# Per-channel scale-and-bias steps of a hybrid mixer kernel, on ScalarE instead of VectorE

## The chip, the cores and the metric

The kernel runs on one core of a Trainium2 chip. The metric is the device time of one execution in microseconds (us); the median of three runs of the kernel before is 2065.13 us (2061.42 to 2069.36). A core has a matrix engine (TensorE, PE in the profile, with its weight loads shown as PEld), a vector engine (VectorE, DVE), an engine for activation functions (ScalarE, ACT), GpSimd (POOL) and a queue that issues most DMAs (SyncE, SP). Each engine executes its own list of instructions strictly in the order of the list, and waits on semaphores for the others.

## The reference, cut to what matters

Two groups of tokens (128 context tokens and 512 latent ones, 640 columns in all) go through two layers. In each layer a normalised input of 1024 features is projected to some 11,800 columns, which feed four mixers (retention, RG-LRU, gated DeltaNet and HGRN2, 4 heads or blocks of 128 channels each, forward and backward); a projection of each, gated, is summed, projected again and added to the input. Two places matter here: the convolutions over four neighbouring tokens, and the gate of HGRN2.

```python
def conv_centred(x, w):
    xp = jnp.pad(x, ((0, 0), (CONV_LEFT, CONV_K - 1 - CONV_LEFT), (0, 0)))
    return sum(xp[:, j:j + n] * w[j] for j in range(CONV_K))
...
xb = conv_centred(bx, lru_conv_w[l]) + lru_conv_b[l]
qkv = jax.nn.silu(conv_centred(jnp.concatenate([cq, ck, cv], -1), gdn_conv_w[l]))
...
k_in = (1.0 - lb) * jax.nn.sigmoid(-zf)
f_gate = lb + (1.0 - lb) * jax.nn.sigmoid(zf)
log_f = jnp.log(jnp.maximum(f_gate, 1e-30))
```

With t = tanh(zf / 2), both gate values are affine in t, with one factor and one addend per channel: k = hb - hb * t and f = ha + hb * t.

## The kernel before, in words

Features lie on the 128 partitions and tokens along the row, so a tile of one head is 128 x 640 (128 x 644 with the padding of a convolution). The large products (projection, branch and output) run as jobs of 128 output features: a 512 KB weight tile is loaded, split into a rounded part (`whi`, an ACT copy, L359) and a rest (`wlo`, a DVE subtraction, L361), and multiplied in 48 matmuls, 24 for columns 0 to 383 and 24 for columns 384 to 639 (L376, output `pj`, two PSUM buffers in turn). After each half ACT copies the result out of PSUM, often through a tanh (`mg`, `p_df` at L521, `p_dq` and `p_bz` at L515, where DVE then multiplies at L516), or plainly (`p_ck`, `p_cq`, `p_cv`, `p_bx` at L507 to L510).

Between these matmuls stand the small ones of the mixers (`m`, L297, and transposes, L301). Two lanes run beside the jobs: the DeltaNet heads in one, the HGRN2, retention and RG-LRU heads in the other. The kernel is written as generators that yield where a result has to come back; a clock that counts PE work decides which lane goes on next. The order of each engine's list is then set by the tile framework's scheduler, which moves instructions against each other within the bounds of their dependencies. All engines' lists are fixed before the run.

The change touches `conv` (L848), which starts with a product by one factor per channel (L851; L853 with an addend too) and adds three more taps on DVE (L855), and the function `after` inside `hgrn_in` (L1114), which makes the two gate tiles from the tanh `th` at L1117 and L1118 and then bounds one of them from below (L1119). `conv` is called 12 times in a layer for DeltaNet and 4 times for RG-LRU (16 in a layer, 32 in all), `after` 8 times in a layer (16 in all). Other names in the rows: `gS`, `vk`, `r`, `gvn` are tiles of the DeltaNet chain over five blocks of tokens (L1066 to L1096), whose products with `cs` and `kt` alternate with DVE and ACT steps; `lt` is a gate tile of RG-LRU (L1376), `lxh` and `lgh` the operands of its matmuls; `dfull` is a tile of the DeltaNet inverse, `mjunk` a dot product of the next layer's modulation; `wide` and `wpart` belong to the first jobs of a layer.

Of the kernel before, what the change touches and what calls it, by code (L numbers as in the profile page):

```python
# [26 lines left out]
AF = mybir.ActivationFunctionType  # L27
OP = mybir.AluOpType
# [10 lines left out]
CONVW = SC + 3 + SS + 1  # L39
# [40 lines left out]
def hybrid_kernel(ctx: ExitStack, tc: tile.TileContext, I, O):  # L80
    nc = tc.nc
    V, G, A, PE = nc.vector, nc.gpsimd, nc.scalar, nc.tensor
# [69 lines left out]
    def UP(shape=None, dt=F32, name="p"):  # L152
        return up.tile([128, T] if shape is None else shape, dt, tag="pu", name=name, bufs=NPU)
# [44 lines left out]
    def small(w, name):  # L198
        return cp.tile([128, w], F32, name=name)
# [13 lines left out]
    def softplus(out, x, w):  # L213
# [11 lines left out]
    lg, cpos, cneg, gbh, ea, ha, hb, hbn, ghg, ghh = (small(w, n) for n, w in (  # L225
        ('lg', 16), ('cpos', 16), ('cneg', 16), ('gbh', 32), ('ea', 16), ('ha', 16), ('hb', 16), ('hbn', 16), ('ghg', 2), ('ghh', 2)))
# [547 lines left out]
    def layer(l, hh, hl):  # L774
# [6 lines left out]
        def proj_to(S, key, name, i, evac, shape=None, after=None):  # L781
            def run(hi, lo):
                x = UP(shape, name="p_" + name)
                yield from product(hi, lo, hh, hl, evac(x), halves=halves)
                if after:
                    after(x)
                S[key] = x
            return Job(I['w_in'][l, CIDX[name, i]], run, cost=2 if name == 'df' else 1)
# [59 lines left out]
        def conv(xp, wcol, dst, bias=None):  # L848

            if bias is None:  # L850
                V.tensor_scalar(dst[:, :CONVW], xp[:, :CONVW], wcol(0), None, op0=OP.mult)  # L851
            else:
                V.tensor_scalar(dst[:, :CONVW], xp[:, :CONVW], wcol(0), bias, op0=OP.mult, op1=OP.add)  # L853
            for j in (1, 2, 3):
                V.scalar_tensor_tensor(dst[:, :CONVW], xp[:, j:j + CONVW], wcol(j), dst[:, :CONVW],  # L855
                                       op0=OP.mult, op1=OP.add)
# [4 lines left out]
        def gdn_conv(h, S, nm):  # L861
            cs = U([128, PADW], name="cs")
            widx = {'cq': 0, 'ck': 4, 'cv': 8}[nm] + h
            conv(S.pop(nm), lambda j: P('gconv_w', l, 12 * j + widx, 1), cs)
            free(1)
            th = U([128, PADW], name="cth")
            A.activation(th[:, :CONVW], cs[:, :CONVW], AF.Tanh, scale=0.5)
            V.scalar_tensor_tensor(cs[:, :CONVW], th[:, :CONVW], 1.0, cs[:, :CONVW], op0=OP.add, op1=OP.mult)
            return cs
# [242 lines left out]
        def hgrn_in(h, S):  # L1112
            def gates(d):
                def after(th):  # L1114
                    c = 8 * l + 4 * d + h
                    k = S['k', d] = UP(name="hk%d" % d)
                    V.tensor_scalar(k, th, hbn[:, c:c + 1], hb[:, c:c + 1], op0=OP.mult, op1=OP.add)  # L1117
                    V.tensor_scalar(th, th, hb[:, c:c + 1], ha[:, c:c + 1], op0=OP.mult, op1=OP.add)  # L1118
                    V.tensor_scalar(th, th, 1e-30, None, op0=OP.max)  # L1119
                return after  # L1120
            return [proj_to(S, 'q', 'dq', h, ev_silu2)] + \
                [proj_to(S, ('f', d), 'df', 4 * d + h, ev_tanh, after=gates(d)) for d in range(2)] + \
                [proj_to(S, 'v', 'di', h, ev_copy)]
# [220 lines left out]
        def lru_mix(c, S):  # L1344
            yield lambda: 'x' in S
            xb = U([128, PADW], name="lxb")
            conv(S['x'], lambda j: P('conv_w', l, 4 * j + c, 1), xb, bias=P('conv_b', l, c, 1))
            free(1)
            gr = U([128, 256], name="lgr")
# [481 lines left out]
```

## Time and profile before

| | |
|---|---|
| median of three runs | 2065.13 us |
| the profiled execution | 2065.96 us, of which the span of the profile is 2063.8 us |
| PE busy | 2026.3 us, 98% of the span |
| PEld busy | 1967.7 us, 95% |
| DVE busy | 1401.8 us, 68% |
| ACT busy | 950.3 us, 46% |
| POOL busy | 77.5 us, 4% |

Shares are averages over the span. Matmuls overlap in the records, and the ends of matmuls are modelled, so how fast PE really goes is read from how many matmuls stand in a stretch of time, not from the busy share alone. What an engine waited for is named by the semaphore that came last.

### The profile page before, as it was taken

The numbers are of one execution on the slowest core, as the hardware profiler recorded it, in microseconds if no ns is written. First come the engines' busy times: TensorE is split into PE (matmuls) and PEld (weight loads), VectorE is DVE, ScalarE is ACT, GpSimd is POOL, SyncE is SP. The second block draws the span as 40 slices with busy tenths as digits, with TensorE's granted clock in tenths as the row PEclk, the third lists the DMA queues.
The fourth block names the chain that finished last, engine by engine and source line by source line (L and its number), as shares of the span: only waits on it lengthen the run. The fifth ranks groups of instructions, "written<-read, shape, count | busy, mean of one in ns | idle before, by whom it ended". The sixth has DMA issues, their size and how long they took to land.

```text
span 2063.8 us, 42790 instructions
## 1 busy us (share of the span) xinstructions
PE 2026.3 (98%) x17362; PEld 1967.7 (95%) x17362; DVE 1401.8 (68%) x3164; ACT 950.3 (46%) x2036; POOL 77.5 (4%) x195
## 2 busy tenths in 40 slices
PE   7999999999999999999999999999999999999997
PEld 5999999999999999999989999999999999999997
DVE  5799998757756954458568656945784686552764
ACT  4443365456537445422344437444643654372221
POOL 0000000001000000000000000000100000000000
PEclk9999999999999999999999999999999999999999
DMA  8236643223323232455422322232332233243632
GB/s 322 80 128 193 187 150 93 93 94 100 100 76 104 84 107 94 143 190 179 144 73 92 94 81 92 92 97 69 123 93 77 78 118 93 96 153 117 212 130 94
DMA packets 133305, 244.20 MB, mean 118 GB/s; under 512 B 44068, under 2 KB 60148, under 8 KB 132980
## 3 DMA queue, kind: packets, MB, share of 16 engines
q1 hardware_dynamic: 131956, 238.85, 35.6%
q8 instruction: 136, 2.23, 0.5%
q10 hardware_dynamic: 1152, 2.62, 0.3%
q14 instruction: 61, 0.50, 0.1%
HBM read 204.15 MB, written 37.27 MB: 117 GB/s over the span
## 4 chain that ended last, share of the span: by engine, by line
PE 89%; DMA 3%; DVE 3%; ACT 3%; issue 1%; SPq 1%; POOL 0%; DVEq 0%; ACTq 0%
PE pj L376 74%; PE m L297 13%; PE m L301 2%; PE wide L384 1%; DMA dct<-d_dr 1%; DMA wss<-in_w_ss 1%; DVE mjunk L630 1%; DMA d_dr<-sW 0%; ACT dfull L1002 0%; DVE wlo L361 0%; ACT whi L359 0%; DMA R<-gc 0%; DMA par<-in_params 0%; ACT lt L1376 0%; DMA tab<-in_tables 0%
## 5 line engine op out<-in xcount | busy, mean ns | idle before, releaser
L376 PE MATMUL pj<-hh,whi 128*128 128x256 f32 (+2 forms) x2896 | 912.9, 315 | 2.9 <-DVE p_dz L516 1.1
L376 PE MATMUL pj<-hl,whi 128*128 128x256 f32 (+2 forms) x2896 | 905.9, 313 | 0.1
L376 PE MATMUL pj<-hh,wlo 128*128 128x256 f32 (+1 forms) x2880 | 899.4, 312 | 0.0
L376 PEld LDWEIGHTS pj<-hh,whi 128*128 128x128 f32 (+1 forms) x2896 | 547.5, 189 | 9.0 <-issue 1.5
L376 PEld LDWEIGHTS pj<-hl,whi 128*128 128x128 f32 (+1 forms) x2896 | 547.8, 189 | 3.7 <-issue 2.0
L376 PEld LDWEIGHTS pj<-hh,wlo 128*128 128x128 f32 x2880 | 545.5, 189 | 3.2 <-issue 1.9
L359 ACT ACTIVATE whi<-wraw 128x1024 fp32r<-128x1024 f32 x230 | 243.4, 1058 | 302.6 <-PE pj L376 259.6
L361 DVE TENSOR_TENSOR wlo<-wraw,whi 128x1024 fp32r<-128x1024 f32 x228 | 278.7, 1223 | 141.1 <-ACT whi L359 137.6
L376 PE MATMUL pj<-bl,whi 128*128 128x384 f32 (+1 forms) x512 | 158.1, 309 | 0.0
L376 PE MATMUL pj<-bh,whi 128*128 128x384 f32 (+1 forms) x512 | 158.0, 309 | 0.0
L376 PE MATMUL pj<-bh,wlo 128*128 128x384 f32 (+1 forms) x512 | 157.5, 309 | 0.0
L376 PEld LDWEIGHTS pj<-bl,whi 128*128 128x128 f32 x512 | 96.3, 188 | 0.0
L376 PEld LDWEIGHTS pj<-bh,whi 128*128 128x128 f32 x512 | 96.3, 188 | 0.0
L376 PEld LDWEIGHTS pj<-bh,wlo 128*128 128x128 f32 x512 | 96.2, 188 | 0.0
L521 ACT ACTIVATE mg<-pj 128x384 f32<-128x384 f32 (+1 forms) x128 | 54.9, 429 | 80.3 <-PE pj L376 76.8
L630 DVE SCALAR_TENSOR_TENSOR mjunk<-wm,cs 128x512 bf16<-128x512 f32 x128 | 87.9, 686 | 2.2 <-DMA wm<-in_w_mod 1.6
L1376 ACT ACTIVATE lt<-m,gbh 64x322 f32<-64x322 f32 x128 | 67.3, 526 | 31.2 <-PE m L297 29.7
L376 PE MATMUL pj<-yl,whi 128*128 128x256 f32 (+1 forms) x256 | 78.9, 309 | 0.0
L376 PE MATMUL pj<-yh,whi 128*128 128x384 f32 (+1 forms) x256 | 78.8, 310 | 0.0
L376 PE MATMUL pj<-yh,wlo 128*128 128x256 f32 (+1 forms) x256 | 78.0, 309 | 0.0
L543 ACT ACTIVATE junk<-m 128x128 bf16<-128x128 f32 x160 | 44.5, 278 | 61.0 <-PE m L297 53.9
L967 DVE TENSOR_TENSOR sW<-sW,sLt 128x126 f32<-128x126 f32 (+22 forms) x248 | 62.8, 253 | 8.5 <-POOL sW L960 3.7
(394 smaller groups left out, 2892.0 us busy)
## 6 DMA issues: line engine op xcount, KB each, us to landing
wraw<-in_w_in SPq DMA_DIRECT2D x184, 512.0 KB
mg<-mg SPq DMA_DIRECT2D x96, 320.0 KB
wm<-in_w_mod SPq DMA_DIRECT2D x64, 256.0 KB
wraw<-in_w_branch SPq DMA_DIRECT2D x32, 512.0 KB
R<-gc SPq DMA_DIRECT2D x32, 320.0 KB
braw<-br SPq DMA_DIRECT2D x32, 320.0 KB
wss<-in_w_ss SPq DMA_DIRECT2D x32, 256.0 KB
wraw<-in_w_out SPq DMA_DIRECT2D x16, 512.0 KB
```

The lines of the kernel that those rows point to most:

```text
L297: return PE.matmul(out, lhsT, rhs, **k)
L301: return PE.transpose(out, in_, idn)
L359: A.activation(hi, raw, AF.Copy)
L361: behind(lambda: (lo_on or j.lo_on or V).tensor_sub(lo, raw, hi.bitcast(F32)), after)
L376: PE.matmul(ps[:m, :b - a], w[:, k0 + k], r[k][:, a:b], start=(k + n == 0), stop=(k == nk - 1 and n == len(ops) - 1))
L384: PE.matmul(ps[:m, :b - a], w[:, k], r[k][:, a:b], start=(k + n == 0), stop=(k == nk - 1 and n == (2 if lo else 1)))
L521: A.activation(dst[:, a:b], ps, AF.Tanh, scale=0.5)
L543: A.activation(junk, src3[:, t, :], AF.Square, accum_out=ss[:, t:t + 1])
L630: V.scalar_tensor_tensor(junk, w, 1.0, cs[2 * g + a], op0=OP.mult, op1=OP.mult, accum_out=macc[l][:, c, 2 * g + a:2 * g + a + 1])
L967: V.tensor_tensor(tv, X3[:, :m, i:i + 1].to_broadcast([128, m, n]), L3[:, i:i + 1, i + 1:].to_broadcast([128, m, n]), op=OP.mult)
L1376: A.activation(gts[g][i:i + 64, sx], ps[64 * g:64 * g + 64, b], AF.Tanh, scale=0.5, bias=gbh[i:i + 64, bi + 4 * g:bi + 4 * g + 1])
```

## The change

The first tap of `conv` and the two affine steps of `after` are taken from DVE's list and put on ACT's, as activations Copy or Identity with scale and bias from the same columns. The other three taps and the bound stay on DVE.

```diff
         def conv(xp, wcol, dst, bias=None):
             if bias is None:
-                V.tensor_scalar(dst[:, :CONVW], xp[:, :CONVW], wcol(0), None, op0=OP.mult)
+                A.activation(dst[:, :CONVW], xp[:, :CONVW], AF.Copy, scale=wcol(0))
             else:
-                V.tensor_scalar(dst[:, :CONVW], xp[:, :CONVW], wcol(0), bias, op0=OP.mult, op1=OP.add)
+                A.activation(dst[:, :CONVW], xp[:, :CONVW], AF.Identity, scale=wcol(0), bias=bias)
...
                 def after(th):
-                    V.tensor_scalar(k, th, hbn[:, c:c + 1], hb[:, c:c + 1], op0=OP.mult, op1=OP.add)
-                    V.tensor_scalar(th, th, hb[:, c:c + 1], ha[:, c:c + 1], op0=OP.mult, op1=OP.add)
+                    A.activation(k, th, AF.Identity, scale=hbn[:, c:c + 1], bias=hb[:, c:c + 1])
+                    A.activation(th, th, AF.Identity, scale=hb[:, c:c + 1], bias=ha[:, c:c + 1])
                     V.tensor_scalar(th, th, 1e-30, None, op0=OP.max)
```

The scheduler orders every engine's list anew, so small matmuls, evacuations and splits stand at other places too. Three places follow.

ACT's list at the start of layer 0, as a piece of the difference: `p_cq` is the second projection's evacuation, `beta` a small tile of DeltaNet gates.

```order
 L508 ACTIVATE p_cq<-wide 128x256
 L510 ACTIVATE p_cq<-wide 128x256
+L851 ACTIVATE cs<-p_ck,par 128x644
 L810 ACT_TABLE_LOAD
 L810 ACTIVATE beta<-m_767 128x40
```

The first tap of the first convolution now stands on ACT, behind the evacuations of `p_cq` and ahead of a table load.

PE's list in the chain of the first DeltaNet head, before: `m_2697` and `m_2700` are the products from which the two directions' new `gS` are made, `m_2730` the first product that reads one of them.

```order
L297 MATMUL m_2697<-vk,kt 128x128
L376 MATMUL pj<-hh,whi 128x256
L376 MATMUL pj<-hl,whi 128x256
L376 MATMUL pj<-hh,wlo 128x256
L376 MATMUL pj<-hh,whi 128x256
L376 MATMUL pj<-hl,whi 128x256
L376 MATMUL pj<-hh,wlo 128x256
L297 MATMUL m_2700<-vk,kt 128x128
L297 MATMUL m_2730<-gS,cs 128x128
L297 MATMUL m_2934<-lxh,lgh 128x322 x2
```

The same place now, from `m_2700` on.

```order
L297 MATMUL m_2700<-vk,kt 128x128
L376 MATMUL pj<-hl,whi 128x384
L376 MATMUL pj<-hh,wlo 128x384
L376 MATMUL pj<-hh,whi 128x384
L376 MATMUL pj<-hl,whi 128x384
L376 MATMUL pj<-hh,wlo 128x384
L301 MATMUL m_2738<-ident,fo 128x128 x5
L376 MATMUL pj<-hh,whi 128x384
L376 MATMUL pj<-hl,whi 128x384
L376 MATMUL pj<-hh,wlo 128x384
L297 MATMUL m_2730<-gS,cs 128x128
```

Before, `m_2730` followed `m_2700` at once; now eight projection matmuls and five transposes stand between them, and the RG-LRU matmul behind has moved away.

ACT's list at the same place, now: the evacuation of a gate projection `p_df`, then what follows it up to the next split of weights.

```order
L521 ACTIVATE p_df<-pj 128x256
L853 ACTIVATE lxb<-p_bx,par 128x644
L1355 ACTIVATE lgh<-lgr 128x256
L1117 ACTIVATE hk_3280<-p_df,hb,hbn 128x640
L1118 ACTIVATE p_df<-p_df,ha,hb 128x640
L1076 ACTIVATE gvn<-m_2790,b_997 128x128
L359 ACTIVATE whi<-wraw 128x1024
```

Before, the steps at L853, L1117 and L1118 stood on DVE, and between `p_df` and `whi` ACT had `lgh` and two steps `gvn`; now three of the moved steps stand there in a row with `lgh` and one `gvn`.

## Rows read from the trace of the kernel before

**Rows 1.** Page, busy time of each engine (share of the span), instructions.
```profile
PE 2026.3 (98%) x17362; PEld 1967.7 (95%) x17362; DVE 1401.8 (68%) x3164; ACT 950.3 (46%) x2036; POOL 77.5 (4%) x195
```
**Rows 2.** Busy time by stretches of the span; first row names the columns.
```profile
core 0: us, PE busy (x) PEld busy (x) DVE busy (x) ACT busy (x) POOL busy (x), PEclk, DMA share, GB/s
60.00:1035.00 975.00, 970.15 (x8307) 946.01 (x8307) 705.97 (x1652) 454.47 (x985) 35.25 (x83) 1.00 0.38 124
1050.00:2040.00 990.00, 988.02 (x8444) 962.34 (x8443) 637.25 (x1376) 461.01 (x987) 35.39 (x93) 1.00 0.32 103
0.00:60.00 60.00, 42.46 (x442) 36.19 (x443) 36.34 (x87) 27.18 (x50) 3.58 (x16) 0.97 0.82 296
1035.00:1050.00 15.00, 12.52 (x84) 10.76 (x82) 9.50 (x23) 5.70 (x11) 1.77 (x1) 1.00 0.26 94
2040.00:2064.00 24.00, 13.19 (x92) 12.44 (x90) 12.70 (x30) 1.88 (x4) 1.55 (x2) 0.80 0.31 110
```
**Rows 3.** Chain that ended last, in order of time: start us, us, what.
```profile
63.12 7.06 PE pj L376 x48
```
**Rows 4.** Timeline of PE: start us, us, instruction [idle before <-releaser].
```profile
54.17 0.69 PE L376 MATMUL pj<-hh,wpart 128*128 128x384 f32 x1 [2.12 <-ACT p_cq L508]
...
253.71 0.49 PE L297 MATMUL m<-gS,cs 128*128 128x128 f32 x2 [1.63 <-DVE gS L1095]
...
285.84 1.00 PE L301 MATMUL m<-ident,p_di 128*128 128x128 f32 x5 [1.32 <-ACT lt L1376]
...
394.10 0.38 PE L376 MATMUL pj<-hh,whi 128*128 128x256 f32 x1 [1.02 <-DVE p_dq L516]
```
**Rows 5.** Busy time by stretches (columns of rows 2), behind three of those idles.
```profile
54.20:57.60 3.40, 3.40 (x11) 3.40 (x12) 1.66 (x4) 2.62 (x4) 0.00 (x0) 0.51 0.33 127
255.60:259.00 3.40, 3.40 (x12) 3.40 (x12) 3.40 (x8) 0.00 (x0) 0.00 (x0) 0.51 0.71 249
286.30:289.70 3.40, 3.40 (x14) 3.38 (x13) 3.37 (x9) 3.24 (x8) 0.00 (x0) 0.51 0.75 227
```
**Rows 6.** Groups by line, DVE: count | busy us, mean ns | idle before.
```profile
L1118 DVE TENSOR_SCALAR p_df<-p_df,hb,ha 128x640 f32<-128x640 f32 x16 | 9.7, 609 | 0.1
L1117 DVE TENSOR_SCALAR hk<-p_df,hbn,hb 128x640 f32<-128x640 f32 x16 | 9.7, 608 | 0.0
...
L853 DVE TENSOR_SCALAR lxb<-p_bx,par 128x644 f32<-128x644 f32 x8 | 4.9, 608 | 0.0
...
L851 DVE TENSOR_SCALAR cs<-p_cq,par 128x644 f32<-128x644 f32 x8 | 4.4, 549 | 0.0
```
**Rows 7.** Groups by line, ACT, of about the same width.
```profile
L867 ACT ACTIVATE cth<-cs 128x644 f32<-128x644 f32 x24 | 17.8, 742 | 15.7 <-DVE cs L855 15.4
L1383 ACT ACTIVATE la<-lt,cneg 128x644 f32<-128x644 f32 x16 | 14.8, 925 | 0.3
...
L1309 ACT ACTIVATE rkt<-m,r_kd 128x640 f32<-128x640 f32 x8 | 6.4, 797 | 6.3 <-PE m L301 6.2
```
**Rows 8.** Waits: engine, line, waited for: us in total, times, longest.
```profile
ACT whi L359 <- PE pj L376: 259.6, 123, 6.0
```
**Rows 9.** Timeline of DVE ahead of the idle at 253.71.
```profile
245.52 0.61 DVE L853 TENSOR_SCALAR lxb<-p_bx,par 128x644 f32<-128x644 f32 x1
...
248.59 0.61 DVE L1117 TENSOR_SCALAR hk<-p_df,hbn,hb 128x640 f32<-128x640 f32 x1
...
251.38 0.61 DVE L1118 TENSOR_SCALAR p_df<-p_df,hb,ha 128x640 f32<-128x640 f32 x1
...
253.31 0.35 DVE L1095 SCALAR_TENSOR_TENSOR gS<-gS,etot,m 128x128 f32<-128x128 f32 x1
```
**Rows 10.** Timeline of ACT ahead of the idle at 394.10.
```profile
387.65 1.05 ACT L1002 ACTIVATE dfull<-dct,con 128x160 f32<-128x160 f32 x3
...
391.40 1.06 ACT L359 ACTIVATE whi<-wraw 128x1024 fp32r<-128x1024 f32 x1
392.36 0.37 ACT L515 ACTIVATE p_dq<-pj 128x256 f32<-128x256 f32 x1
```

## The prediction

> **What bounds the kernel now.** I read the page's busy times first: PE is busy 98% of the span, DVE 68%, ACT 46% [rows 1]. That share alone proves little, since matmuls overlap in the records, so I take a pace: 48 projection matmuls (24 of 384 columns, 24 of 256) in a row of the chain that ended last take 7.06 us, 147 ns each [rows 3]. Such jobs fill most of the span, and no order of the other engines makes 48 of them shorter than where nothing interrupts them. Next the stretches [rows 2]: PE is idle 60.00 - 42.46 = 17.5 us at the head, where weights and inputs arrive, 15.00 - 12.52 = 2.5 us between the layers, and some 10.6 us at the end, in the final norm. In the 1965 us that remain, where every moved instruction but one stands, it is idle 975.00 - 970.15 = 4.85 and 990.00 - 988.02 = 1.98, together 6.8 us. Last, the idles themselves [rows 4]: in the body two exceed 1.1 us, 1.63 us until a `gS` of DVE and 1.32 us until `lt` of ACT; a third of 1.02 us waits for the DVE half of an evacuation; and one of 2.12 us, at the start of layer 0, waits for ACT's evacuation of `p_cq`. Behind three of the four PE runs 3.4 us at a granted clock of 0.51, the level of 1.2 GHz, after 2.4 GHz before [rows 5]. Half speed for 3.4 us costs 1.7 us, so such an idle costs twice what it seems. All that the change can give back in the body is 6.8 + 2 x 1.7 = 10.2 us; with the start of layer 0 (2.1 + 1.7) it is 14.0 us.
>
> **What is removed.** 24 first taps at 549 ns, 8 with an addend at 608, 16 + 16 gate steps at 609 and 608 [rows 6]: 13.2 + 4.9 + 19.5 = 37.6 us of DVE, 2.7% of its 1402 us. PE's own instructions stay as they are. Beside PE nearly all of this is hidden, so it is worth what it shortens of PE's idles that DVE ends.
>
> There is one such place with moved instructions in it. In the 8 us ahead of the idle at 253.71, three of the moved steps (L853, L1117, L1118, 0.61 us each, 1.8 us in all) stand in DVE's list ahead of the `gS` that ends the wait, and none of these rows shows an idle before it: DVE has a queue there [rows 9]. PE had nothing between the product `m_2700` and `m_2730`, which reads `gS`. In the changed lists the three have left DVE, and between the two products PE has eight matmuls of 384 columns and five transposes. At 147 ns for the mean width the eight alone take 1.2 us, over 1.6 us with the transposes (five transposes take 1.00 us in [rows 4]). The 1.63 us should go, and with it the slow clock behind: -3.3 us. What is late next there is `gvn` on ACT, which now stands behind `lgh` and two gate steps.
>
> The idle at 54.17 stays: the first tap stands behind both evacuations of `p_cq` on ACT, so it comes too late to lengthen this wait and does nothing to shorten it. The idle at 285.84 waits for ACT, which is given more to do; I leave it, and that at 394.10, at their size.
>
> **What is added.** ACT gets 24 Copies with one factor read per partition, and 8 + 32 = 40 Identities with factor and addend. The trace of before has the nearest rows: 742 ns at 644 columns with neither, 925 ns with both, and 797 ns for one factor from PSUM at 640 [rows 7]. The Identities are the second kind, so 40 x 0.925 = 37.0 us at most; the Copies lie between the first two, 17.8 to 22.2 us, and I take 0.83, near the third, 20.0 us. That is 57 us (47.5 if all ran as the cheapest row, 59.2 as the dearest), and ACT's 950 us become 1007, 49% of the span. None of it is on the path by itself: ACT waits 259.6 us in all for PE before its splits of weights alone [rows 8], so the cover is its own idle time. It is gone where ACT is late for an evacuation. PE has two output buffers, so an evacuation is late when it comes more than one half after the matmuls that filled it: 256 / 640 of 7.06, 2.8 us, for the shorter half. Two gate steps behind each other are 1.85 us, below this; with a split of weights of 1.06 us in front [rows 10] they are 2.9 us, about at it. In the list shown, the next evacuation follows the gate steps only after `gvn`, a split and more, but PE has its small matmuls there too.
>
> So I expect a few new waits, not one for each of the 64 moved steps. Bounded from both sides: below nothing, if the new order also loses the waits at 285.84 and 394.10, 1.32 + 1.7 + 1.02 = -4.0 us; above, an ACT list that repeats the case of [rows 10], where ACT worked from 387.65 to 392.36 ahead of an evacuation and PE lost 1.02 us, once for each of 16 gate pairs, +16.3 us. Between them I take one new idle of the size of those seen, 1.3 us, as most of ACT's time is free.
>
> The sum against the profiled execution (2065.96 us, span 2063.8, 2.2 us around it, 0.8 above the median of the runs): 2065.96 - 3.3 + 1.3 = **2064.0 us**.
>
> **Two rules of the Trainium skill.** [Rows 6, 7] show the same affine step at 0.61 us on DVE and about 0.92 on ACT. "ScalarE: Activation LUTs", section "Rules for kernel authors", says to use VectorE, not ScalarE, for add and mul, and the trace agrees on the price. By that rule the change is a loss of 57 - 37.6 = 19 us of engine time; where ACT's time was PE's time this would be 2085 us, a rival below.
>
> PEld, the weight loads, is busy 1967.7 us [rows 1], so 96 us of the span have none. "Perfetto Trace Analysis", section "Identifying the Most-Contended Engine", calls matmul busy time a poor measure and wants headroom judged by weight loads and arithmetic rate; by that reading up to 96 us could be won, by the gaps between matmuls 37. Time without a weight load but with a matmul is not time in which PE waits for DVE or ACT, and only such waits can the change touch, so the sum goes by the gaps.
>
> **The rivals.**
> - Nothing moves but the place of the waits: `m_2730` waits no more, and `gvn`, later by the two gate steps, makes PE wait as long elsewhere in the same chain. For it: the chain alternates PE, DVE and ACT. Against it: PE's list was rearranged for the new order. 2065.96 - 3.3 + 3.3, with the new idle of 1.3: 2067 us.
> - Slower: ACT, strictly in order, holds back evacuations. The place is the gate pair behind `p_df`, 16 times; the price is the 1.02 us of [rows 4] for each, 16.3 us; it decides once a split (1.06) and a pair (1.85) stand ahead of an evacuation within a half of 2.8 us. 2082 us. With idles long enough for the slow clock each costs 1.02 + 1.7, and six are enough for 2082. Against it: ACT idles half the time.
> - Slower by engine time: 2085 us, as above. Against it: two of the four large idles wait for ACT, 3.4 us together [rows 4], though ACT has 950 us of work [rows 1].
> - Clearly faster: DVE's relief and the new order empty the body of waits and of slow clock, and the start of layer 0 too: 2065.96 - 14.0 = 2052 us. Against it: two of the four waits are ACT's.
> - The change does not do what it says, because a Copy or Identity brings a table load with it (such a load stands in the first list shown, ahead of `beta`). The list of the changed kernel has no load beside the moved steps, and the same number in all, 35; I give it nothing.
>
> **How the numbers follow.** The forecast has 0.60, the moved wait 0.20, held-back evacuations 0.11, engine time 0.03, the clearly faster case 0.06. About 0.5%, 10.3 us, is what can be told from no change here, so faster means below 2054.8 and slower above 2075.4. The forecast's own range is 2057 (all of the body's 6.8 us gone with one slow stretch kept) to 2073 (the one wait gained, and three or four new ones with slow clock, 3.3 each). The first two cases lie within 0.5% but for a few hundredths: same 0.78. Slower takes the two slower rivals and the forecast's upper tail, 0.16, faster 0.06. The range that should hold 8 times in 10 is 2056 to 2077: it holds the first two cases and the near part of the slower one.
>
> **What would show it.** PE busy stays at 2026 us within 4; ACT rises to about 1000 us, DVE falls to about 1364; the Copies show 0.83 us, the Identities 0.92. The wait of PE for `gS` near 253 us is gone, and the clock there stays at 2.4 GHz; that for `p_cq` near 54 us is there. Body idle is 4 to 9 us. The slower rival would show as PE waiting for `p_df`, `mg` or the evacuation after a gate pair, at many heads, with more stretches of 0.51. I am wrong if PE's idle in the body exceeds 15 us, or if the time leaves 2055 to 2075 with PE's busy time unchanged; if the busy time itself changes, the pace was not what I took it for.

## The result, and the profile after

The changed kernel takes 2079.73 us, the median of six runs (2076.04 to 2082.87); the kernel before took 2064.75 in six runs beside it. The ratio is 1.0070 (95% interval 1.0059 to 1.0080): 15 us slower, where 2064.0 and at most 2077 were forecast. The profiled execution of the changed kernel is its shortest, 2076.04 us with a span of 2074.2. Against the profiled 2065.96 of before that is 10.1 us, and the rows below speak of these; of the other 5 us there is no trace.

The page's first part, as [rows 1]:

```profile
PE 2026.2 (98%) x17362; PEld 1966.4 (95%) x17362; DVE 1368.3 (66%) x3100; ACT 998.4 (48%) x2100; POOL 76.6 (4%) x195
```

PE does the same work in the same time, 2026.2 against 2026.3 us. DVE has 33.5 us less, ACT 48.1 more. So the whole difference of these two executions is time in which PE stands still: 2074.2 - 2026.2 = 48.0 us against 37.5. The second layer starts 3.8 us later than before and the final norm 10.0 us later, so the bounds of the stretches are moved with them (columns of [rows 2]):

```profile
60.00:1038.82 978.82, 967.98 (x8301) 944.23 (x8301) 687.02 (x1615) 478.58 (x1015) 35.62 (x83) 1.00 0.38 123
1053.82:2050.02 996.20, 989.50 (x8445) 962.31 (x8444) 622.00 (x1344) 483.59 (x1019) 34.51 (x93) 1.00 0.32 102
```

PE's idle time in the body is 978.82 - 967.98 = 10.84 and 996.20 - 989.50 = 6.70, together 17.5 us, against 6.8 before. The groups of the moved instructions, now on ACT:

```profile
L1117 ACT ACTIVATE hk<-p_df,hb,hbn 128x640 f32<-128x640 f32 x16 | 14.7, 921 | 0.3
L1118 ACT ACTIVATE p_df<-p_df,ha,hb 128x640 f32<-128x640 f32 x16 | 14.7, 918 | 0.3
L853 ACT ACTIVATE lxb<-p_bx,par 128x644 f32<-128x644 f32 x8 | 7.3, 918 | 0.0
L851 ACT ACTIVATE cs<-p_ck,par 128x644 f32<-128x644 f32 x8 | 6.7, 832 | 0.0
```

They last as forecast, 0.92 us with factor and addend and 0.82 to 0.83 with a factor alone. With the other two groups of L851 (6.6 us each) they sum to 56.6 us; the engine's busy time grew by less. Neighbours overlap at their ends (in a row below a step of 1.04 us starts at 1357.56 and the next one at 1358.51).

What PE waited for, grouped (us in total, times, longest); first the kernel before, then the changed one:

```profile
PE pj L376 <- ACT mg L521: 0.3, 1, 0.3
```
```profile
PE pj L376 <- ACT mg L521: 3.5, 5, 1.0
PE pj L376 <- ACT rsw L1275: 2.4, 2, 1.6
PE m L301 <- ACT lt L1376: 2.0, 1, 2.0
PE pj L376 <- DVE p_bz L516: 1.9, 1, 1.9
PE pj L376 <- ACT p_df L521: 1.6, 3, 0.8
```

`mg`, `rsw`, `p_df` and `p_bz` are evacuations of projections; all but `p_bz` end on ACT, and in `p_bz` a DVE product follows ACT's step. Summed over this view, PE's waits that ACT ends rise from 5.8 to 16.4 us, those that DVE ends from 9.2 to 9.6; so the added idle time is nearly all ACT's. Some of these idles in PE's timeline, with the four that answer to [rows 4] (that of 394.10 is gone):

```profile
53.55 0.69 PE L376 MATMUL pj<-hh,wpart 128*128 128x384 f32 x1 [2.11 <-ACT p_cq L508]
...
214.50 0.44 PE L376 MATMUL pj<-hh,whi 128*128 128x384 f32 x1 [1.86 <-DVE p_bz L516]
...
254.54 0.49 PE L297 MATMUL m<-vk,kt 128*128 128x128 f32 x2 [0.50 <-DVE vk L1079]
255.74 0.41 PE L297 MATMUL m<-lxh,lgh 64*128 64x322 f32 x2 [0.70 <-ACT lxh L490]
...
285.19 0.44 PE L301 MATMUL m<-ident,p_di 128*128 128x128 f32 x1 [2.01 <-ACT lt L1376]
...
450.36 0.44 PE L376 MATMUL pj<-hh,whi 128*128 128x384 f32 x1 [0.87 <-ACT mg L521]
...
1360.46 0.38 PE L376 MATMUL pj<-hh,whi 128*128 128x256 f32 x1 [1.56 <-ACT rsw L1275]
```

What stands ahead of three of them, first DVE's list for 214.50, then ACT's for 450.36 and 1360.46:

```profile
212.48 0.69 DVE L630 SCALAR_TENSOR_TENSOR mjunk<-wm,cs 128x512 bf16<-128x512 f32 x1 [0.45 <-DMA wm<-in_w_mod]
...
213.09 0.89 DVE L1053 TENSOR_TENSOR R<-cs,R 128x128 f32<-128x128 f32 x2
213.90 0.55 DVE L516 SCALAR_TENSOR_TENSOR p_bz<-p_bz,pj 128x384 f32<-128x384 f32 x1
```
```profile
444.58 0.92 ACT L1117 ACTIVATE hk<-p_df,hb,hbn 128x640 f32<-128x640 f32 x1
445.53 0.92 ACT L1118 ACTIVATE p_df<-p_df,ha,hb 128x640 f32<-128x640 f32 x1
446.47 1.28 ACT L1389 ACT_TABLE_LOAD   x1
447.76 0.74 ACT L1389 ACTIVATE lt<-lt 128x644 f32<-128x644 f32 x1
448.52 1.28 ACT L521 ACT_TABLE_LOAD   x1
449.82 0.49 ACT L521 ACTIVATE mg<-pj 128x384 f32<-128x384 f32 x1
```
```profile
1354.35 1.39 ACT L1002 ACTIVATE dfull<-dct,con 128x160 f32<-128x160 f32 x4 [1.93 <-DMA dct<-d_dr]
...
1357.56 1.04 ACT L359 ACTIVATE whi<-wraw 128x1024 fp32r<-128x1024 f32 x1
1358.51 0.36 ACT L496 ACTIVATE p_aq<-pj 128x256 f32<-128x256 f32 x1
1358.89 0.38 ACT L1275 ACTIVATE rsw<-pj 64x256 f32<-64x256 f32 x1
1359.29 0.74 ACT L1005 ACTIVATE dn<-dcn,con 64x160 f32<-64x160 f32 x2
1360.04 0.38 ACT L1275 ACTIVATE rsw<-pj 64x256 f32<-64x256 f32 x1
```

Read the second piece from below: PE can go on at 450.36 because the copy of `mg`, begun at 449.82, was over at 450.31, and it stands behind 5.2 us of ACT work without a gap, two moved steps first. This is what the slower rival described. The other two pieces are not. At 214.50 PE waits for DVE's product on the 384 columns of `p_bz`, which stands in DVE's list behind a step that waited for a DMA; ACT was done with these columns at 212.24. At 1360.46 the evacuation `rsw` stands behind ACT steps that waited for a DMA, and no moved step is among them.

So I followed each wait of the body that ACT ends back in ACT's list, to the last place where ACT itself stood idle for more than 0.15 us. There are 17 such waits, 12.9 us in all (4 and 2.2 us before). Moved steps stand in the stretch behind 5 of them, 2.8 us together; 7, 5.7 us together, begin with a step that waited for a DMA (one of them is among the 5). For 10.1 us of the 12.9 no moved step is directly ahead; that one acts by way of another engine is not excluded by this.

With the change the scheduler also set every list anew. Below, one such order of all lists is called a deal. Counted in the traces, with buffer numbers and table loads left out, 9675 of 17,362 matmuls of PE and 151 of 2001 steps of ACT have the same place number as before. For ACT that overstates it, as 64 new rows shift all that follow: in the longest order common to both, 14,996 and 1653 remain. The trace alone can't say whether the moved steps or the new deal made the waits.

### The profile page after: what moved, and what is told of

It reads as the page before. It is cut to its first block, busy times and chain, and to the rows that moved or that the text cites. A ratio compares the mean times of both kernels' runs of the same rounds, so it can differ in the third digit from the quotient of the medians.

```text
span 2074.2 us, 42784 instructions
## 1 busy us (share of the span) xinstructions
PE 2026.2 (98%) x17362; PEld 1966.4 (95%) x17362; DVE 1368.3 (66%) x3100; ACT 998.4 (48%) x2100; POOL 76.6 (4%) x195
## 4 chain that ended last, share of the span: by engine, by line
PE 81%; ACT 6%; DMA 5%; DVE 4%; issue 2%; SPq 1%; POOL 0%; DVEq 0%; ACTq 0%; POOLq 0%
PE pj L376 67%; PE m L297 12%; PE m L301 2%; ACT whi L359 1%; DMA R<-gc 1%; DMA dct<-d_dr 1%; PE wide L384 1%; DMA d_dr<-sW 1%; ACT lt L1376 1%; DMA tab<-in_tables 1%; DVE mjunk L630 1%; DMA wss<-in_w_ss 1%; DVE wlo L361 1%; SPq L981 1%; ACT dfull L1002 0%
## 5 line engine op out<-in xcount | busy, mean ns | idle before, releaser
L521 ACT ACTIVATE mg<-pj 128x384 f32<-128x384 f32 (+1 forms) x128 | 54.5, 429 | 77.3 <-PE pj L376 72.1
```

Of the source, the lines that this page charges most:

```text
L521: A.activation(dst[:, a:b], ps, AF.Tanh, scale=0.5)
```

## The experiments

Theories: **Q**, the 48 us of work added to ACT's queue cost about in proportion; **L**, any new deal of the lists costs, whatever ACT does, since before's pacing constants fit its own deal; **H**, the results now cross from ACT to DVE, and somebody waits; **B**, it is ACT's steps that wait for a DMA, with evacuations behind them. "Idle" is PE's in the two stretches of the body, with bounds moved as above; it is 6.8 us before. All ratios are to runs of the kernel before on the same chip, with 95% intervals.

| run | median us | ratio | ACT us | idle us |
|---|---|---|---|---|
| change | 2079.7 | 1.0070 [1.0059, 1.0080] | 998 | 17.5 |
| e1 convolutions alone | 2071.1 | 1.0034 [1.0022, 1.0046] | 974 | 15.2 |
| e2 gate steps alone | 2074.9 | 1.0046 [1.0031, 1.0062] | 979 | 18.4 |
| e3 before, both neutral edits | 2067.2 | 1.0010 [1.0000, 1.0020] | 950 | 9.1 |
| e9 before, neutral edit 1 | 2071.6 | 1.0030 [1.0018, 1.0041] | 950 | 10.8 |
| e10 before, neutral edit 2 | 2071.1 | 1.0033 [1.0021, 1.0045] | 951 | 10.0 |
| e8 before, DVE's steps left out | 2070.3 | 1.0034 [1.0021, 1.0046] | 952 | 13.8 |
| e11 before, 80 copies to DVE | 2069.7 | 1.0024 [1.0014, 1.0034] | 919 | 12.7 |
| e4 before, 64 unread steps on ACT | 2074.3 | 1.0041 [1.0027, 1.0055] | 1002 | 15.8 |
| e16 e4, both neutral edits | 2076.1 | 1.0058 [1.0046, 1.0070] | 1004 | 17.0 |
| e17 e4, neutral edit 1 | 2080.9 | 1.0096 [1.0078, 1.0115] | 1005 | 17.8 |
| e12 change, both neutral edits | 2080.5 | 1.0081 [1.0068, 1.0093] | 1003 | 23.5 |
| e18 change, neutral edit 1 | 2078.0 | 1.0065 [1.0053, 1.0077] | 1001 | 18.0 |
| e7 change, 64 unread steps more | 2094.8 | 1.0147 [1.0131, 1.0164] | 1048 | 29.2 |
| e5 change, 80 copies to DVE | 2074.1 | 1.0050 [1.0036, 1.0063] | 972 | 14.0 |
| e6 change, DMA-waiting steps to DVE | 2071.6 | 1.0038 [1.0025, 1.0050] | 962 | 16.4 |
| e13 change's lists, 32 table loads fewer | 2075.9 | 1.0059 [1.0045, 1.0074] | 956 | 16.0 |
| e14 before's lists, 44 table loads more | 2088.8 | 1.0122 [1.0107, 1.0137] | 1008 | 23.3 |
| e15 before's lists, 32 table loads fewer | 2062.1 | 0.9990 [0.9981, 0.9999] | 908 | 6.1 |

**The halves (e1, e2).** Each is the diff above with the other half left as before.

> The first taps of the convolutions alone on ScalarE (32 steps, about 27 us of ACT), the gate steps left on VectorE. Theory Q (queue: added ACT time stands ahead of evacuations, so PE waits for ACT in proportion to it): about 27/57 of the +15 us, so +7 us, 2072; PE's idle in the body released by ACT about 7 to 8 us, against 2.5 before and 13.2 with the whole change. Theory L (lists: any change makes the scheduler deal all lists anew, and the loss is a matter of chance): anywhere from -8 to +15, and the two halves need not add up to +15.

> The gate steps alone on ScalarE (32 steps, about 30 us of ACT), the first taps left on VectorE. Theory Q: about 30/57 of +15, so +8 us, 2073; PE's idle released by ACT about 8 us. Theory L: anywhere from -8 to +15, not adding up with the convolutions alone.

They add up: 0.34 + 0.46 = 0.80%, the whole 0.70%. Neither the taps nor the gate pairs alone are the culprit, and both times lie near what Q expected. L had allowed anything from -8 to +15 us, so this does not decide between them.

**Neutral deals (e3, e9, e10).** The same work on each engine, with evacuations swapped between ACT and DVE; e9 has the first edit, e10 the second, e3 both:

```
-                if d:                      # L1306, rkt's two evacuations
+                if not d:
...
-    PL0, PL1, PL2 = 'AVAV', 'AVAV', 'AV'   # L148
+    PL0, PL1, PL2 = 'VAVA', 'VAVA', 'VA'
```

> The kernel before with a swap that leaves each engine's time as it was: of pairs of equal copies out of PSUM or of equal small tiles, the one that was on ScalarE goes to VectorE and the other way round (the HGRN2 score blocks and the two retention key tiles). The lists are dealt anew. Theory Q: no change, 2065 within 4 us, PE's idle in the body within 3 us of 6.8. Theory L: a change of the size of the effect, 8 us or more either way.

> The kernel before with one neutral edit: of the two evacuations of the retention keys' transposes, the one that ScalarE took goes to VectorE and the other way round. ScalarE's work stays at 950 us. A theory in which only ScalarE's added time counts: 2064 us (+-2). A theory in which any other deal of the instruction lists loses the settings that were fitted to the old one: 2066 to 2071, with ScalarE-released idle of TensorE of 5 us or more (before: 2.5).

> The kernel before with another neutral edit: the copies into the HGRN2 score tile swap engines in turn (VAVA for AVAV). ScalarE's work stays at 950 us. Added-time theory: 2064 us. Lists dealt anew: 2066 to 2071.

These were to be blanks, and they are not: 0.10, 0.30 and 0.33% slower at 950 us of ACT. e3 alone would have fitted Q, and missed the 8 us that L named; e9 and e10 lie at the upper edge of what a new deal was expected to cost. The edit of e9 touches 8 evacuations on each engine, yet only 1549 of ACT's 2001 steps keep their place number, 1834 their order. What PE waits for in e9 has the look of the changed kernel's row:

```profile
PE pj L376 <- ACT mg L521: 3.2, 5, 1.5
```

So waits like those of the changed kernel, `mg` among them, come also with a new deal that adds nothing to ACT.

**Work added, work left out (e4, e7, e8).** e4 and e7 run the 64 moved steps once more on ACT, into a tile that nobody reads; e8 takes the first tap's weight as 1, and leaves its addend and the second gate step out.

```
+                idle_act(xp, CONVW, wcol(0))            # e4, e7: A.activation into xtra
...
+                    idle_act(th, T, hbn[:, c:c + 1], hb[:, c:c + 1])
...
-                V.tensor_scalar(dst[:, :CONVW], xp[:, :CONVW], wcol(0), None, op0=OP.mult)   # e8
...
-                    V.tensor_scalar(th, th, hb[:, c:c + 1], ha[:, c:c + 1], op0=OP.mult, op1=OP.add)
```

> The kernel before with VectorE's steps left in place, and the same 64 activations executed by ScalarE in addition, into a tile that nobody reads: ACT's load of the change without VectorE's relief and without new dependencies of others on ACT. Theory Q: the load alone is the cause, so +15 us or a little more, about 2080, with PE's idle released by ACT about 13 us. A third theory, H (hand-over: the convolutions' and gates' chains now pass through ACT, which delays the mixers that PE waits for), expects less than half of it, under +7 us, since nobody waits for the added steps. Theory L: anything from -8 to +15.

> The whole change and the 64 activations a second time, into a tile that nobody reads: ScalarE's added load doubled to about 105 us, the rest as in the change. Theory Q: the loss of the change plus that of the load alone, 15 + 8.5, so 2087 to 2090, PE's idle released by ACT about 20 to 25 us. Theory B or L: within 5 us of 2080, as what holds the evacuations is not the load.

> The kernel before with the first taps and the second gate step left out altogether (the convolution's second tap then adds the unscaled input in their place, and the bound works on the bare tanh): VectorE's relief of about 28 us without any load on ScalarE; part of the computation is missing. Theory Q: VectorE's relief is worth little, 2060 to 2065. Theory L (lists dealt anew are what costs): could be 2057 to 2073, with PE's idle released by ACT as likely up as down.

e8 shows no gain from DVE's relief: with less work and no step moved the time is 0.34% longer, at the upper end of the neutral deals and above the 2065 that Q allowed. A gain of a few us could hide in the spread of the deals. e4 shows that the load costs though nobody reads its result; its 0.41%, 8.5 us, lies between the 15 us that Q and the less than 7 that H had named. It is not wholly free of hand-overs: DVE overwrites `th` in place, so its gate step has to wait until ACT has read it. e7 shows that a second load costs another 0.77%, 16 us; its Q sum was too low.

**ACT relieved in the change (e5, e6).** e5 puts the copies `hkst` (L1180, L1181) on DVE, e6 the three steps that wait for a DMA (L957, L1002, L1005).

```
-                    A.activation(hv(kst, 0), hv(kf, 0), AF.Copy)   # e5, and the same for half 1
+                    V.tensor_copy(hv(kst, 0), hv(kf, 0))
...
-            A.activation(sLt[64:], sW[64:, ::-1], AF.Copy)         # e6, and L1002, L1005 alike
+            V.tensor_copy(sLt[64:], sW[64:, ::-1])
```

> The whole change, and in return 80 other copies of ScalarE (the two halves of the HGRN2 key tile, 38.7 us) put on VectorE: ScalarE's load is back near that of before (about 960 us). Theory Q (added ScalarE time stands ahead of evacuations): PE's idle released by ACT falls from 13 to 3 to 7 us, time 2063 to 2069. Theory H (hand-over: chains of the convolutions and gates now pass through ScalarE): the 6 us that added load alone did not explain stay, so 2071 or more. Theory B (blocking: evacuations stand behind a ScalarE step that waits for a DMA, and it is these that PE waits for): those steps are still there, so 5 us or more of the loss stay, about 2071.

> The whole change, and in return the ScalarE steps that wait for a DMA in the DeltaNet inverse (the reversed copy into sLt, the masked copies dfull and dn; about 42 us) put on VectorE: ScalarE is relieved by about as much as with the key-tile copies on VectorE, and no evacuation stands behind such a wait any more. Theory Q: as the key-tile version, 2063 to 2069. Theory B: better than the key-tile version by 4 us or more, at or below before, 2060 to 2065; VectorE is then the engine that is held, and evacuations with a VectorE half (p_dz, p_bz) may show it. Theory H: 2071 or more.

By the ratios 4 and 7 us of the 15 come back, less than Q expected of either (2063 to 2069). e6, which B named, gives back more, but not down to the 2060 to 2065 of B, and it also takes 36 us off ACT against 26; per us the two are about even (4.1 / 26 and 6.6 / 36, 0.16 and 0.18). B is not shown, though 7 of the 17 waits followed back above do begin behind a DMA. Both times fit H. By then every line of thought could claim the rest, since e5 and e6 are new deals too.

**The other way round (e11, e12).** e11 is e5's edit on the kernel before; e12 the change with both neutral edits.

> The kernel before with the 80 stacking copies of HGRN2's keys (L1180, L1181) on VectorE: ScalarE falls by 38 us to about 912, VectorE rises by 20 to 35. If ScalarE's time alone decides, with the slope of 0.25 us per us that the loads of 950 to 1048 us showed: 2055 to 2064 us, and less ScalarE-released idle than the 2.5 us of before. If any other deal of the lists costs: 2066 to 2072 in spite of the lighter ScalarE.

> The change with the two neutral edits in it (the score tile's copies and the retention keys' evacuations swapped between the engines): ScalarE at 998 us as in the change. Added-time theory: 2078 to 2082, as the change. If the particular deal of the lists makes part of the 15 us: another time by several us, 2070 to 2076 or 2084 to 2088.

Taking 31 us off ACT makes the kernel before slower, 1.0024: Q alone falls. Another deal of the change is no better, 1.0081, as Q expected: L alone doesn't explain it either.

**The same lists, another ACT time (e13, e14, e15).** A table load (1.283 us) is put in where two functions on ACT want different tables, after the order is settled. So a function can be swapped with every other row of every list in its place; in the traces the order of all five engines is the same, table loads left out. e13 and e15 take a square for the square root of L1389, which removes 32 loads; e14 computes the first key copies of three levels as a square root at scale 0.

```
-                A.activation(tr, tr, AF.Sqrt)                       # e13 (change), e15 (before)
+                A.activation(tr, tr, AF.Square)
-                    A.activation(hv(kst, 0), hv(kf, 0), AF.Copy)    # e14, at levels 0, 2 and 4
+                    A.activation(hv(kst, 0), hv(kf, 0), AF.Sqrt, scale=0.0)
```

> The change with the square root of L1389 replaced by a square (its values differ, it takes 742 ns as before): every instruction list stays as it is in the change, and the 32 table loads of 1.283 us that Tanh and Sqrt forced on each other go, 41 us. ScalarE about 957 us, near the 950 of before. If ScalarE's added time alone makes the 15 us: 2064 to 2068, ScalarE-released idle of TensorE near 2.5 us. If the new deal of the lists alone makes it: 2078 to 2081. If both, as two neutral deals at 950 us (2071) suggest: 2069 to 2073.

> The kernel before with 48 of its 80 first key copies (L1180, at three levels of the scan) as a square root at scale 0 (the stacked keys' first halves are zero there): all lists as before, and 44 more table loads, 56 us; ScalarE about 1007 us. Added time alone: 2078 to 2080. Lists alone: 2063 to 2067. If before's lists stand only because the pacing was fitted to them, and take load like other lists (7 to 8 us for 48): 2071 to 2074.

> The kernel before with the square root of L1389 replaced by a square: all lists as before, 32 table loads (41 us) fewer, ScalarE about 909 us. Added time with the slope of 0.25 us per us below 950 too: 2055. If before's ScalarE queue is already short enough, its 2.5 us of ScalarE-released idle is all there is: 2061 to 2065.

The pages' first part, of e13 and of e14:

```profile
PE 2027.0 (98%) x17362; PEld 1969.1 (95%) x17362; DVE 1368.3 (66%) x3100; ACT 956.4 (46%) x2068; POOL 76.5 (4%) x195
```
```profile
PE 2033.1 (97%) x17362; PEld 1972.2 (95%) x17362; DVE 1403.1 (67%) x3164; ACT 1007.7 (48%) x2080; POOL 77.1 (4%) x195
```

e13 has ACT within 6 us of before, and it is still 0.59% slower: 42 us less on ACT give back 2 us of 15 by the ratios, 4 by the medians, and the intervals of e13 and of the change overlap. The time falls into none of the three ranges named for it. The wait at `p_bz` stands there as it did; first PE, then DVE in e13:

```profile
214.65 0.44 PE L376 MATMUL pj<-hh,whi 128*128 128x384 f32 x1 [2.28 <-DVE p_bz L516]
```
```profile
212.62 0.69 DVE L630 SCALAR_TENSOR_TENSOR mjunk<-wm,cs 128x512 bf16<-128x512 f32 x1 [0.90 <-DMA wm<-in_w_mod]
...
213.24 0.89 DVE L1053 TENSOR_TENSOR R<-cs,R 128x128 f32<-128x128 f32 x2
214.05 0.55 DVE L516 SCALAR_TENSOR_TENSOR p_bz<-p_bz,pj 128x384 f32<-128x384 f32 x1
```

The DMA wait in DVE's list is 0.45 us longer than in the change, and PE's wait 0.42: no ACT step shows in this part of the loss.

In before's lists 42 us less are worth 1.5 us, but 57 us more, in lumps of 1.28, cost 25. The expectation for Q was 2078 to 2080: a miss, too low. The table loads ahead of L521, a tanh that evacuates a projection, first in e14, then in the kernel before:

```profile
L521 ACT ACT_TABLE_LOAD x19 | 24.4, 1283 | 1.4 <-PE pj L376 1.1
```
```profile
L521 ACT ACT_TABLE_LOAD x9 | 11.5, 1283 | 1.4 <-PE pj L376 1.3
```

Ten more evacuations than before have a load directly ahead, but this is not the main part: PE's waits for `mg` grow to 2.2 us only, and e15, which has none of the nine loads, gains 1.5 us. The largest new wait is for `sq`, a DeltaNet step and no evacuation, 0.32 us before; ACT's list ahead of it, with PE's row first:

```profile
112.09 0.27 PE L297 MATMUL m<-ones,sq 128*128 128x1 f32 x1 [3.40 <-ACT sq L922]
```
```profile
106.82 1.28 ACT L1181 ACT_TABLE_LOAD   x1
...
108.97 1.28 ACT L619 ACT_TABLE_LOAD   x1
110.26 1.15 ACT L619 ACTIVATE cth<-cs 128x512 f32<-128x512 f32 x2
111.32 0.72 ACT L922 ACTIVATE sq<-cs 128x644 f32<-128x644 f32 x1
```

So ACT's sum alone does not set the price; here the work stands ahead of something that PE waits for. Of the 22.8 us that e14's profiled span is longer, 6.8 are more busy time of PE (2033.1 against 2026.3); ahead of the final norm the granted clock stood at 1.2 GHz for 20.5 us, against 10.2 before.

**Read or not read (e16, e17, e18).** Two more deals of e4's unread load and one more of the change, by the neutral edits above.

> As e4 (before, with 64 activations more on ScalarE into a tile that nobody reads; VectorE keeps its steps), dealt another way by the two neutral edits. ScalarE about 1001 us. If ScalarE's load and a new deal make the change's loss, with or without readers: about as the change's two deals, 2076 to 2081 (0.7 to 0.8%). If part of it is that VectorE now waits for the moved steps' results: 2070 to 2075, as e4 (0.41%).

> As the run before, with the retention keys' edit alone: a third deal of the same unread load. Load and deal: 2076 to 2081. Readers matter: 2070 to 2075.

> The change with the retention keys' edit alone: a third deal of the change, ScalarE about 998 us. If the change costs 0.7 to 0.8% in any deal: 2078 to 2081. If its first two deals were bad draws: 2071 to 2076.

Unread, the load costs 0.41, 0.58 and 0.96%; read, 0.70, 0.81 and 0.65%. The means are 0.65 and 0.72%, and the two sets overlap: H is not needed. The waits of DVE for the unread steps, in e4, e16 and e17 in turn, do not follow the loss either:

```profile
DVE p_df L1129 <- ACT xtra L853: 3.9, 5, 1.3
```
```profile
DVE p_df L1129 <- ACT xtra L853: 0.7, 1, 0.7
```
```profile
DVE p_df L1129 <- ACT xtra L853: 0.8, 2, 0.7
```

All three medians fall where the load was expected to cost in any deal, e16 and e18 at the lower edge.

Put together: five deals without added work on ACT (e3, e8, e9, e10, e11) cost 0.10 to 0.34%, 0.26% in the mean; six with 64 steps more (the change, e4, e12, e16, e17, e18) cost 0.41 to 0.96%, 0.68%. So of the 14 us of that mean, 5.4 come with a new deal alone, and 8.7 with the 64 steps in ACT's list, 0.14 us for each. By the scatter within the two groups the 8.7 may be anything from 5 to 13 (95%). Runs with the same neutral edits say the same: the 64 steps add 0.48 and 0.71% to e3 (e16, e12), 0.66 and 0.35% to e9 (e17, e18). That they merely upset the lists more does not fit: e4 keeps 1896 of ACT's 2001 rows in order and costs 0.41%, e8 keeps 1591 and costs 0.34. For the change alone the split is an estimate by these means. How the steps come to cost it is open: waits with a moved step directly ahead make 2.8 us in the change, and the rest is not traced to them. No version here beats the kernel before with the same outputs.

## Why the prediction was wrong

**The bound was right.** PE's busy time stayed, 2026.2 us, so all that happens between the two profiled executions is in PE's idle time.

**The wait that goes: half right.** The `gS` wait of 1.63 us is gone, and in its place stand 0.50 us for `vk`, the next in the chain (I named `gvn`), and 0.70 us for `lxh`, of RG-LRU. The clock there is full, as said:

```profile
255.00:258.50 3.50, 2.80 (x17) 2.57 (x17) 3.50 (x9) 1.34 (x4) 0.00 (x0) 1.00 0.27 104
```

That makes 0.4 + 1.7 = 2.1 us instead of 3.3.

**The added work: durations right, cover wrong.** The failed step is "I take one new idle of the size of those seen, 1.3 us, as most of ACT's time is free". The body's idle grew by 10.7 us, nearly all of it in waits that ACT ends (2.2 before, 12.9 now), and the six deals with the load cost 8.7 us more than those without. An engine that is 46% busy in the mean was late where PE needed it, in 17 places of the body. Only at 5 of them, 2.8 us, do moved steps stand directly ahead, as at 450.36; elsewhere it is other steps of the new order, at 6 places behind a DMA. Why the load makes PE wait there is open. ACT's free time didn't even shrink; ACT's wait for PE before its splits, 259.6 us in [rows 8], is this in the changed kernel:

```profile
ACT whi L359 <- PE pj L376: 276.3, 130, 6.0
```

A price near the measured one was in the list of rivals: "ACT, strictly in order, holds back evacuations", 2082 us, at a chance of 0.11. Its size came true and its places only in part: waits for `p_df` are 3 and not 16, `mg` and `rsw` have more, and no stretch of slow clock was added. As some 5 us of the loss go with a new deal alone, by the means above, that the number fits is in part luck. My reason against it, that ACT idles half the time, does not hold by e13 and e14: 42 us off the sum give back 2 to 4 us, 57 us at bad places cost 25.

**What the sum left out.** "I leave it, and that at 394.10, at their size" took the rest of the lists as fixed. They were not: the `lt` wait rose from 1.32 to 2.01 us, that at 394.10 went, and `mg`, `rsw`, `p_bz`, `p_df`, nowhere large before, came. The neutral edits price this at 0.10 to 0.33%, 2 to 7 us, always a loss. I had shown two places of the order and asked what moved there; that 348 of ACT's 2001 rows left their order should have told me that the waits elsewhere were drawn again. I put the lower bound at a gain of 4.0 us by this; none of the 15 other new deals measured was a gain. That the pacing constants fit before's deal alone would explain it, but no run changed them, so this is not shown.

**The other rivals.** Engine time, 2085 us, is not far by number but wrong in kind: e8 takes DVE's work away and shows no gain, and e13 shows that ACT's time is not additive. The rule beside it (the Trainium skill, "ScalarE: Activation LUTs", section "Rules for kernel authors": add and mul on VectorE) pointed the right way, and the runs agree with its advice, not with a price by engine time. Table loads are 35 in both, as said.

## What to carry to other kernels

On an in-order engine that also evacuates PSUM for a busy TensorE, do not take the engine's mean share of idle time as cover for added work: here 64 steps of 0.9 us on a 46% busy engine cost some 9 us in the mean of six deals. Follow each wait back in the list of the engine that ends it before naming a cause; most here did not stand behind the moved steps. Where the lists are dealt by a scheduler with hand-set pacing, count how many rows keep their order; if many do not, add the price of a new deal, which two or three neutral edits measure (2 to 7 us here), before believing any gain or loss of that size. To separate the two, change a duration that the deal doesn't look at, such as a table load.

## What was not expected of the hardware

An idle of 1.3 us or more was not followed by slow clock each time. Behind 1.86 us at 214.50 and 1.56 us at 1360.46 the granted clock stayed at 2.4 GHz, behind 2.01 us at 285.19 it fell to 1.2 (columns of [rows 2]):

```profile
214.50:218.00 3.50, 3.50 (x20) 3.50 (x21) 3.50 (x7) 0.39 (x2) 0.00 (x0) 1.00 0.32 98
285.20:288.60 3.40, 3.40 (x16) 3.40 (x17) 2.98 (x9) 3.22 (x6) 0.00 (x0) 0.51 0.77 246
1360.50:1364.00 3.50, 3.50 (x30) 3.50 (x30) 3.40 (x7) 2.95 (x6) 0.00 (x0) 1.00 0.48 150
```

In e13 the wait at the same `p_bz`, 2.28 us there, was followed by it:

```profile
215.50:219.00 3.50, 3.50 (x14) 3.50 (x13) 3.50 (x6) 0.00 (x0) 0.00 (x0) 0.55 0.28 81
```

So the price of 1.7 us on top of such an idle, which the prediction used, holds for some of them; what decides was not tried.
